# Loads of the conditioning rows moved from SP's queue to POOL's, and the updates of x in three feed-forwards done by adding transfers

## The chip, the cores and the metric

One core of one Trainium2 chip. Measured is the device time in microseconds (us) of one execution; lower is better. Work goes to TensorE (PE, with PEld for its weight loads), VectorE (DVE), ScalarE (ACT), GpSimd (POOL) and to DMA transfers, which a queue of SyncE (SP) or of POOL issues. Each of these runs its own instructions strictly in order.

## The reference, cut to what matters

Two layers over 640 tokens (128 context, 512 latent) of width 1024. Each layer is a feed-forward, a token mixing and a second feed-forward; every one of the three has its own shift, scale and gate, which come from a conditioning vector:

```python
mods = (silu(cond) @ w_ada + b_ada).reshape(cond.shape[0], 9, 1, 1024)
sh1, sc1, g1, sh2, sc2, g2, sh3, sc3, g3 = [mods[:, i] for i in range(9)]
...
h = modulate(rmsnorm(x, p['norm_ffn1']), sh1, sc1)
x = x + 0.5 * g1 * swiglu(h, p['w_ffn1_in'], p['w_ffn1_out'])
```

`swiglu(h, w_in, w_out)` is `(silu(g) * u) @ w_out` with `g, u` the halves of `h @ w_in`, 2816 columns each. `cond` differs between context and latent tokens, so every row of `w_ada` is multiplied with two vectors.

## The kernel before, in words

x lies transposed in SBUF as eight tiles `x` of 128 channels by 640 tokens. Every product is made three times, with a high and a low half of both factors: `Weights.piece` (L168 to L176) rounds a loaded weight tile `raw` to `hi` on ACT (L174) and takes the rest `lo` on DVE (L175). There are four `hi` and four `lo` buffers and nine `raw` buffers; SP loads the `raw` tiles (L159).

**A feed-forward** (`ffn`, L532) goes through 22 column pairs in five parts of 5, 5, 4, 4 and 4 (`PARTS`). In a part first come the *pairs* (`pair`, L596): seven products of combined blocks (PE, L503), with four sums of weight tiles (DVE, L608), evictions and the activation. Then comes the *out part*: for each of the eight x tiles `out` (L644) multiplies the part's activations with `w_out` (PE, L135) and `x_update_joined` (L523) adds the product times the gate to x, with two DVE instructions (L528, 128 and 512 columns). This text calls the four feed-forwards F1 to F4 (layer 0 first, layer 0 second, layer 1 first, layer 1 second), the pairs of their parts P1 to P5 and the out parts O1 to O5. In the first part of F1 two pairs are done in another way (`plain_pair`), and in the last out part of each feed-forward the next norm's tiles are made as well (`nx.tile`).

**The conditioning rows.** `ada_steps` (L258) makes 128 rows of the product with `w_ada` in one *step*: a 512 KB load into one of two `wa` buffers (L268) and two DVE instructions with a running sum (L270), one for each conditioning vector. A list of such steps, the `Pump`, is filled ahead of F1, F2 and F3 (`ada_all`), and `tick` (L538) takes a step from it whenever a credit, which grows by 2 times a rate for a pair and by the rate for an x tile, has reached one. `RATES` gives the rate of each feed-forward; F4 has none. There are 132 steps. Written order is not final: a scheduler orders the instructions of each engine when the program is built, so an instruction may stand earlier or later in its engine's row than its place in the code.

The evictions `g` and `u` of a pair, and from the change on the products for x, come from one pool of five buffers, `T` (tiles named `t`). PSUM has two buffers `S` for the products of the out part.

Of the kernel before, what the change touches and what calls it, by code (L numbers as in the profile page):

```python
# [12 lines left out]
AF = mybir.ActivationFunctionType  # L13
ALU = mybir.AluOpType
# [8 lines left out]
POOLD = ()  # L23
SHO = range(8)
SPREAD = 3
RATES = (0.8, 0.8, 0.55)
WLATE = 4
P1A, P0B, P1B = 1, 2, 2
D = 1024
# [3 lines left out]
N = NC + NL  # L33
TX = N + 2
FFN = 2816
NP = 22
# [11 lines left out]
HN = N // 2  # L48
# [3 lines left out]
SEGS = ((0, 0, NC), (1, NC, N))  # L52
# [30 lines left out]
def hybrid_step(ctx: ExitStack, tc: tile.TileContext, x_in, cc_in, cb_in, w_ada0, w_ada, pv_in, lam_in, w_fin, w_fout, w_min, w_mout,  # L83
                cache_in, ident_in, rope_in, cnt_in, sel_in,
                y_out, ngk, ngv, ndk, ndv):
    nc = tc.nc
    V, S, G, PE = nc.vector, nc.scalar, nc.gpsimd, nc.tensor
# [13 lines left out]
    def nm(s):  # L101
        uid[0] += 1
        return f"{s}_{uid[0]}"
# [4 lines left out]
    def T(dt=F32):  # L108
        return tp.tile([128, UW], dt, tag="t", name=nm("t"))
# [11 lines left out]
    def PS():  # L121
        return psS.tile([128, 2, 512], F32, tag="S", name=nm("S"))

    def PH():
        return psH.tile([128, 512], F32, tag="H", name=nm("H"))

    def PF():
        return psF.tile([128, 512], F32, tag="F", name=nm("F"))

    def C(shape, dt=F32, name="c"):  # L130
        n = nm(name)
        return const.tile(shape, dt, tag=n, name=n)
# [5 lines left out]
    x = [C([128, N], name="x") for _ in range(KT)]  # L138
# [11 lines left out]
    def raw_tile():  # L150
        return wp.tile([128, 512], F32, tag="raw", name=nm("raw"), bufs=RAWB)

    def load_raw(src):

        n, r = src.shape[-1], []
        for c in range(0, n, 512):
            w = min(512, n - c)
            t = raw_tile()
            nc.sync.dma_start(t[:, :w], src[:, c:c + w])  # L159
            r.append(t[:, :w])  # L160
        return r

    class Weights:
# [5 lines left out]
        @staticmethod  # L169
        def piece(src, eng=None):  # L170
            n = src.shape[-1]
            hi = wp.tile([128, 512], F32R, tag="hi", name=nm("hi"), bufs=HLB)
            lo = wp.tile([128, 512], F32R, tag="lo", name=nm("lo"), bufs=HLB)
            S.activation(hi[:, :n], src, AF.Copy)  # L174
            (eng or V).tensor_tensor(out=lo[:, :n], in0=src, in1=hi[:, :n], op=ALU.subtract)  # L175
            return hi, lo  # L176
# [45 lines left out]
    mods = [[None] * 18 for _ in range(L)]  # L222

    def bada(l, c):
        b = PV_BADA + l * 72 + 4 * c
        return pv[:, b:b + 4].unsqueeze(2).to_broadcast([128, 4, 2])
# [33 lines left out]
    def ada_steps(l, c):  # L260
        m = []

        def step(b):
            if b == 0:
                m.append(C([128, 4, 2], name="mod"))
            t = sp.tile([128, 1536], F32, tag="KS", name=nm("wa"), bufs=2)
            raw, dump = t[:, :D], t[:, D:].bitcast(mybir.dt.bfloat16)
            nc.sync.dma_start(raw, w_ada[l, 4 * c + b])  # L268
            for i, o in enumerate((dump, raw)):
                V.scalar_tensor_tensor(out=o, in0=raw, scalar=1.0, in1=rows[i], op0=ALU.mult, op1=ALU.mult,  # L270
                                       accum_out=m[0][:, b, i:i + 1])
            if b == 3:
                V.tensor_tensor(out=m[0], in0=m[0], in1=bada(l, c), op=ALU.add)
                mods[l][c] = m[0]

        return [lambda b=b: step(b) for b in range(4)]
# [10 lines left out]
    def gate_tiles(l, sub):  # L287

        if sub == 1:
            return [mods[l][2 * (3 * sub + 2) + h] for h in range(2)]  # L290
        r = []
        for h in range(2):
            t = C([128, 4, 2], name="gate")
            V.tensor_scalar(out=t, in0=mods[l][2 * (3 * sub + 2) + h], scalar1=-0.5, scalar2=None, op0=ALU.mult)
            r.append(t)
        return r
# [199 lines left out]
    def product(ps, piece, act, start):  # L496

        hi, lo = piece
        for k in range(4):
            w0, w1 = hi[:, k * 128:(k + 1) * 128], lo[:, k * 128:(k + 1) * 128]  # L500
            ah, al = act[k][:, 0], act[k][:, 1]
            for p, (w_, a) in enumerate(((w0, ah), (w0, al), (w1, ah))):
                PE.matmul(ps, w_, a, start=start and k == 0 and p == 0, stop=k == 3 and p == 2, skip_group_check=True)  # L503
# [20 lines left out]
    def x_update_joined(d, p, gate):  # L524
        g = gate[d // 4]
        w = p.rearrange("p a b -> p (a b)")[:, 512 - HN:512 - HN + N]
        for c, a, b in SEGS:
            V.scalar_tensor_tensor(out=x[d][:, a:b], in0=w[:, a:b], scalar=g[:, d % 4, c:c + 1], in1=x[d][:, a:b],  # L528
                                   op0=ALU.mult, op1=ALU.add)


    def ffn(l, sub, norm, nxt, pump, prate):  # L532
        wi = w_fin[l * 2 + (0 if sub == 0 else 1)]
# [65 lines left out]
        def pair(i, first):  # L599


            a11, a12 = load_raw(wi[i, 0])
            a21, a22 = load_raw(wi[i, 1])
            s3 = raw_tile()
            piece = Weights.piece

            def add(o, a, b):
                V.tensor_tensor(out=o, in0=a, in1=b, op=ALU.add)  # L608

            A, B, D = PF()[:, :HW], PH()[:, :HW], PS()[:, 0, :HW]  # L610
            g, u = T(), T()
            w = piece(a11)
            product(A, w, norm.get("B11"), True)
            S.activation(g[:, :HW], A, AF.Copy)
            w = piece(a12)
            add(s3, a11, a21)
            add(a21, a21, a22)
            add(a11, a21, a11)
            product(B, w, norm.get("B21"), True)
            if first:  # L620
                norm.stats_sum()
            V.tensor_tensor(out=g[:, :HW], in0=B, in1=g[:, :HW], op=ALU.add)
            w = piece(a11)
            product(A, w, norm.get("N2"), False)
            S.activation(u[:, :HW], A, AF.Copy)
            w = piece(s3)
            add(a12, a11, a12)
            product(D, w, norm.get("T3"), True)
            S.activation(u[:, HW:], D, AF.Copy)
            if first:  # L630
                norm.stats_spread()
            w = piece(a21)
            product(A, w, norm.get("N1"), False)
            V.tensor_tensor(out=u[:, HW:], in0=A, in1=u[:, HW:], op=ALU.add)
            w = piece(a22)
            product(D, w, norm.get("T4"), False)
            V.tensor_tensor(out=u[:, :HW], in0=D, in1=u[:, :HW], op=ALU.add)
            w = piece(a12)
            product(A, w, norm.get("B22"), False)
            V.tensor_tensor(out=g[:, HW:], in0=A, in1=norm.R[:, HW:], op=ALU.mult)  # L640
            V.tensor_tensor(out=g[:, :HW], in0=g[:, :HW], in1=norm.R[:, :HW], op=ALU.mult)
            V.tensor_tensor(out=u, in0=u, in1=norm.R, op=ALU.mult)  # L642
            activation(i, g, u, HN)

        def out(k0, k1, d, gate, nx):
            ps = PS()
            w = load_w(wo[d, :, k0 * 128:k1 * 128])
            mm3(joined(ps), CN, w, acts[k0:k1], range(k1 - k0))
            x_update_joined(d, ps, gate)
            if nx is not None:  # L650
                nx.tile(d)
            tick(1.0)
# [55 lines left out]
        gate = None  # L708
        for k0, k1 in PARTS:
            for i in range(k0, k1):  # L710
                if l == 0 and sub == 0 and i < NPLAIN:
                    plain_pair(i)
                    if i == 0:
                        for k in range(4):
                            norm.late(k)
                else:
                    pair(i, i == 0)
            gate = gate or gate_tiles(l, sub)
            nx = nxt() if k1 == NP else None
            if k1 == NP and nx is None:  # L720
                last_out(k0, k1, gate)
            else:
                for d in ORDER:
                    out(k0, k1, d, gate, nx)
# [677 lines left out]
    nx = FastNorm(0, 0)  # L1402
# [24 lines left out]
    pump = Pump()  # L1427

    def ada_all(l, cs):
        for c in cs:  # L1430
            pump.add(ada_steps(l, c))

    ada_all(0, (4, 5, 8, 9, 6, 7, 10, 11, 14, 15, 12, 13))
    nx = ffn(0, 0, nx, lambda: Norm(0, 1), pump, RATES[0])
    pump.step(1000)
    cache = load_cache(0)
    lambdas()
    nx = mix(0, nx, lambda: FastNorm(0, 2), cache)
    cache = load_cache(1)
    rows = silu_rows()  # L1440
    ada_all(0, (16, 17))
    ada_all(1, (2, 3, 0, 1, 4, 5, 8, 9, 6, 7))
    nx = ffn(0, 2, nx, lambda: (pump.step(8), FastNorm(1, 0))[1], pump, RATES[1])
    pump.step(1000)
    ada_all(1, (10, 11, 14, 15, 12, 13, 16, 17))
    nx = ffn(1, 0, nx, lambda: Norm(1, 1), pump, RATES[2])
    pump.step(1000)
    nx = mix(1, nx, lambda: FastNorm(1, 2), cache)
# [113 lines left out]
```

## Time and profile before

| | |
|---|---|
| runs | 2492.87, 2497.93 and 2497.96 us; median 2497.93 |
| profiled execution | 2492.2 us; its span, first to last instruction, 2490.4 us; mean granted clock 0.977 |
| busy, share of the span | PE 95%, PEld 92%, DVE 85%, ACT 49%, POOL 13% |
| DMA | 280.70 MB, 113 GB/s on the mean; all of it from SP's queue, but for 2.70 MB of instructions |

"Busy" is the time in which an engine has an instruction under way; the shares are means over stages that differ. A window row of the trace gives, for one stretch, each engine's busy time with the number of its instructions, the granted TensorE clock (1.00 is 2.4 GHz), and the mean share and rate of the 16 DMA engines. Where an engine's busy time is as long as the stretch, it had no pause there. The chain that ended last is nearly all PE in the part of the span that the page shows.

### The profile page before, as it was taken

The numbers are of one execution on the slowest core, as the hardware profiler recorded it, in microseconds if no ns is written. First come the engines' busy times: TensorE is split into PE (matmuls) and PEld (weight loads), VectorE is DVE, ScalarE is ACT, GpSimd is POOL, SyncE is SP. The second block draws the span as 40 slices with busy tenths as digits, with TensorE's granted clock in tenths as the row PEclk, the third lists the DMA queues.
The fourth block names the chain that finished last, engine by engine and source line by source line (L and its number), as shares of the span: only waits on it lengthen the run. The fifth ranks groups of instructions, "written<-read, shape, count | busy, mean of one in ns | idle before, by whom it ended". The sixth has DMA issues, their size and how long they took to land. (4 is left out here: it accounts for less than half of the span.)

```text
span 2490.4 us, 42262 instructions
## 1 busy us (share of the span) xinstructions
PE 2360.5 (95%) x15497; PEld 2290.3 (92%) x15497; DVE 2108.2 (85%) x3978; ACT 1213.3 (49%) x2447; POOL 315.2 (13%) x373
## 2 busy tenths in 40 slices
PE   7799999999998999998989999999999989999998
PEld 4798998999988899998979999999998979999997
DVE  5999998867887999999999998778588688767776
ACT  3534333457664634334355344445576565434434
POOL 3100000034233100000030000002422330000002
PEclk8999999999999999999989999999999989999999
DMA  7354443223423144554423453222243112223223
GB/s 267 109 169 139 156 156 117 86 80 122 136 75 123 60 153 125 160 161 147 128 81 104 155 150 96 69 85 85 76 154 105 51 39 80 82 78 97 81 73 98
DMA packets 142671, 280.70 MB, mean 113 GB/s; under 512 B 15360, under 2 KB 33664, under 8 KB 142464
## 3 DMA queue, kind: packets, MB, share of 16 engines
q1 hardware_dynamic: 142464, 278.01, 35.0%
q8 instruction: 122, 2.00, 0.3%
q14 instruction: 85, 0.70, 0.1%
HBM read 263.00 MB, written 14.94 MB: 112 GB/s over the span
## 5 line engine op out<-in xcount | busy, mean ns | idle before, releaser
L174 ACT ACTIVATE hi<-raw 128x512 fp32r<-128x512 f32 (+2 forms) x954 | 569.3, 605 | 874.2 <-PE S L135 359.4
L503 PE MATMUL F<-u,hi 128*128 128x322 f32 x2752 | 634.7, 318 | 33.0 <-ACT hi L174 31.1
L175 DVE TENSOR_TENSOR lo<-raw,hi 128x512 fp32r<-128x512 f32 (+1 forms) x874 | 565.2, 659 | 114.2 <-ACT hi L174 110.4
L135 PE MATMUL S<-u,hi 128*128 128x320 f32 (+3 forms) x2144 | 485.2, 317 | 35.5 <-DVE x L517 12.9
L503 PEld LDWEIGHTS F<-u,hi 128*128 128x128 f32 x2752 | 469.3, 192 | 41.7 <-ACT hi L174 34.3
L503 PE MATMUL F<-u,lo 128*128 128x322 f32 x1376 | 432.9, 315 | 10.5 <-DVE lo L175 10.5
L135 PE MATMUL S<-u,lo 128*128 128x320 f32 (+3 forms) x1776 | 419.3, 312 | 3.2 <-DVE lo L175 2.3
L135 PEld LDWEIGHTS S<-u,hi 128*128 128x128 f32 x2144 | 361.4, 193 | 46.9 <-issue 13.3
L270 DVE SCALAR_TENSOR_TENSOR wa<-wa,sc 128x1024 bf16<-128x1024 f32 (+1 forms) x264 | 323.5, 1233 | 9.7 <-DMA wa<-in_w_ada_dram 6.3
L135 PE MATMUL S<-e,hi 128*128 128x320 f32 (+2 forms) x1408 | 327.8, 310 | 1.1 <-DVE e L197 0.8
L503 PE MATMUL S<-u,hi 128*128 128x322 f32 x1376 | 316.1, 315 | 2.6 <-DVE x L528 2.3
L135 PEld LDWEIGHTS S<-u,lo 128*128 128x128 f32 x1776 | 305.1, 191 | 4.5 <-DVE lo L175 3.3
L503 PEld LDWEIGHTS F<-u,lo 128*128 128x128 f32 x1376 | 267.0, 194 | 13.8 <-DVE lo L175 13.1
L608 DVE TENSOR_TENSOR raw<-raw,raw 128x512 f32<-128x512 f32 x344 | 239.7, 697 | 5.2 <-DMA raw<-in_w_fin_dram 2.1
L135 PE MATMUL F<-u,hi 128*128 128x320 f32 (+1 forms) x1056 | 239.2, 318 | 1.5 <-DVE x L517 0.8
L503 PEld LDWEIGHTS S<-u,hi 128*128 128x128 f32 x1376 | 234.2, 191 | 5.7 <-ACT hi L174 5.0
L135 PEld LDWEIGHTS S<-e,hi 128*128 128x128 f32 x1408 | 236.6, 188 | 2.9 <-DVE e L197 2.5
L503 PE MATMUL S<-u,lo 128*128 128x322 f32 x688 | 215.3, 313 | 1.4 <-DVE lo L175 1.4
L528 DVE SCALAR_TENSOR_TENSOR x<-S,gate,x 128x128 f32<-128x128 f32 (+1 forms) x304 | 152.6, 544 | 53.0 <-PE S L135 52.1
L135 PEld LDWEIGHTS F<-u,hi 128*128 128x128 f32 x1056 | 178.6, 193 | 3.9 <-DVE x L517 0.8
L135 PE MATMUL F<-u,lo 128*128 128x320 f32 (+1 forms) x528 | 157.8, 318 | 0.0
L503 PE MATMUL H<-u,hi 128*128 128x322 f32 x688 | 156.0, 313 | 1.7 <-ACT hi L174 1.7
(229 smaller groups left out, 3032.8 us busy)
## 6 DMA issues: line engine op xcount, KB each, us to landing
raw<-in_w_fin_dram SPq DMA_DIRECT2D x352, 256.0 KB
wa<-in_w_ada_dram SPq DMA_DIRECT2D x132, 512.0 KB
raw<-in_w_fout_dram SPq DMA_DIRECT2D x168, 256.0 KB
raw<-in_w_min_dram SPq DMA_DIRECT2D x72, 256.0 KB
u<-in_w_ada_dram SPq DMA_DIRECT2D x24, 256.0 KB
KS<-kd SPq DMA_DIRECT2D x16, 384.0 KB
raw<-in_w_mout_dram SPq DMA_DIRECT2D x24, 256.0 KB
kd<-t SPq DMA_DIRECT2D x8, 640.0 KB
```

The source lines that it names most:

```text
L135: PE.matmul(out, lhsT, rhs, start=start, stop=stop)
L174: S.activation(hi[:, :n], src, AF.Copy)
L175: (eng or V).tensor_tensor(out=lo[:, :n], in0=src, in1=hi[:, :n], op=ALU.subtract)
L270: V.scalar_tensor_tensor(out=o, in0=raw, scalar=1.0, in1=rows[i], op0=ALU.mult, op1=ALU.mult, accum_out=m[0][:, b, i:i + 1])
L503: PE.matmul(ps, w_, a, start=start and k == 0 and p == 0, stop=k == 3 and p == 2, skip_group_check=True)
L528: V.scalar_tensor_tensor(out=x[d][:, a:b], in0=w[:, a:b], scalar=g[:, d % 4, c:c + 1], in1=x[d][:, a:b], op0=ALU.mult, op1=ALU.add)
L608: V.tensor_tensor(out=o, in0=a, in1=b, op=ALU.add)
```

## The change

Five edits. (1) The 512 KB loads of `ada_steps` are issued by POOL and no longer by SP. (2) In F1, F2 and F3 the out parts O1 to O4 call a new function `x_update_dma`: ACT multiplies the product in PSUM with the gate into a `t` tile (two instructions), and POOL issues a 320 KB transfer from that tile which adds to the x tile in SBUF. O5 and all of F4 keep the two DVE instructions. (3) `RATES` goes from 0.8, 0.8, 0.55 to 0.6, 0.42, 0.6. (4) Four groups of rows (16 steps) go from the list of F2 to that of F3. (5) Ahead of the first gate the pump is run until the gate's rows are there.

```diff
-RATES = (0.8, 0.8, 0.55)
+RATES = (0.6, 0.42, 0.6)
...
-            nc.sync.dma_start(raw, w_ada[l, 4 * c + b])
+            G.dma_start(raw, w_ada[l, 4 * c + b])
...
+    def x_update_dma(d, p, gate):
+        g = gate[d // 4]
+        w = p.rearrange("p a b -> p (a b)")[:, 512 - HN:512 - HN + N]
+        t = T()
+        for c, a, b in SEGS:
+            S.activation(t[:, a:b], w[:, a:b], AF.Copy, scale=g[:, d % 4, c:c + 1])
+        G.dma_start(x[d], t[:, :N], accum_op=ALU.add)
...
-            x_update_joined(d, ps, gate)
+            (x_update_dma if k1 < NP and prate else x_update_joined)(d, ps, gate)
...
+            while gate is None and mods[l][2 * (3 * sub + 2) + 1] is None:
+                pump.step()
             gate = gate or gate_tiles(l, sub)
...
-    ada_all(1, (2, 3, 0, 1, 4, 5, 8, 9, 6, 7))
-    nx = ffn(0, 2, nx, lambda: (pump.step(8), FastNorm(1, 0))[1], pump, RATES[1])
+    ada_all(1, (2, 3, 0, 1, 4, 5))
+    nx = ffn(0, 2, nx, lambda: (pump.step(1000), FastNorm(1, 0))[1], pump, RATES[1])
     pump.step(1000)
-    ada_all(1, (10, 11, 14, 15, 12, 13, 16, 17))
+    ada_all(1, (8, 9, 6, 7, 10, 11, 14, 15, 12, 13, 16, 17))
```

The instructions of DVE, in the order in which the built programs have them, hold this many L270 instructions (two to a step) in each stretch, P1 of F1 with all that stands ahead of it:

| | P1 | O1 | P2 | O2 | P3 | O3 | P4 | O4 | P5 | to the next P1 |
|---|---|---|---|---|---|---|---|---|---|---|
| F1 before | 25 | 14 | 15 | 13 | 13 | 12 | 12 | 0 | 0 | 11 |
| F1 now | 22 | 20 | 11 | 18 | 8 | 16 | 8 | 1 | 0 | 11 |
| F2 before | 6 | 14 | 15 | 13 | 13 | 12 | 13 | 9 | 8 | 3 |
| F2 now | 6 | 19 | 10 | 19 | 8 | 16 | 8 | 16 | 8 | 3 |
| F3 before | 8 | 12 | 11 | 12 | 0 | 0 | 0 | 0 | 0 | 0 |
| F3 now | 8 | 18 | 10 | 0 | 0 | 0 | 0 | 0 | 0 | 0 |

Three places show what moved. The first is DVE in O3 of F1; `lo` is a weight tile of the out part, `wa` a conditioning load with its two vectors `sc_319` and `sc_322`, `x` an x tile. Before:

```order
L175 TENSOR_TENSOR lo_3537<-raw_3534,hi_3536 128x512
L270 SCALAR_TENSOR_TENSOR wa_3566,mod_3528<-wa_3566,sc_319 128x1024
L175 TENSOR_TENSOR lo_3574<-raw_3571,hi_3573 128x512
L528 SCALAR_TENSOR_TENSOR x_82<-S_3495,gate_1256,x_82 128x128
L528 SCALAR_TENSOR_TENSOR x_82<-S_3495,gate_1256,x_82 128x512
L270 SCALAR_TENSOR_TENSOR wa_3566,mod_3528<-wa_3566,sc_322 128x1024
```

and with the change:

```order
L175 TENSOR_TENSOR lo_3622<-raw_3619,hi_3621 128x512
L270 SCALAR_TENSOR_TENSOR wa_4334,mod_4182<-wa_4334,sc_319 128x1024
L175 TENSOR_TENSOR lo_3657<-raw_3654,hi_3656 128x512
L270 SCALAR_TENSOR_TENSOR wa_4334,mod_4182<-wa_4334,sc_322 128x1024
L270 SCALAR_TENSOR_TENSOR wa_4373,mod_4182<-wa_4373,sc_319 128x1024
L175 TENSOR_TENSOR lo_3697<-raw_3694,hi_3696 128x512
```

The two x instructions are gone and conditioning instructions stand in their place, between the same weight tiles.

The second is the queue of loads at the same O3. Before, SP's row (`raw` with `w_fin` are weights of the next pairs):

```order
L268 DMA wa_3529<-in_w_ada_dram 128x1024
L268 DMA wa_3566<-in_w_ada_dram 128x1024
L159 DMA raw_3720<-in_w_fin_dram 128x512
L159 DMA raw_3722<-in_w_fin_dram 128x512
L268 DMA wa_3603<-in_w_ada_dram 128x1024
L268 DMA wa_3640<-in_w_ada_dram 128x1024
```

and with the change POOL's:

```order
L268 DMA wa_4183<-in_w_ada_dram 128x1024
L268 DMA wa_4334<-in_w_ada_dram 128x1024
L538 DMA x_81<-t_3461 128x640
L538 DMA x_85<-t_3496 128x640
L268 DMA wa_4373<-in_w_ada_dram 128x1024
L538 DMA x_82<-t_3535 128x640
L268 DMA wa_4412<-in_w_ada_dram 128x1024
```

SP has only weights there now; on POOL a conditioning load and the addition to an x tile take turns, each behind the one ahead of it.

The third is the start of the program. Before, SP issues the first conditioning loads behind the x tiles and the vectors `sc`, and ahead of the `u` tiles:

```order
L255 DMA sc_319<-in_cb_dram 128x1024
L255 DMA sc_322<-in_cb_dram 128x1024
L268 DMA wa_326<-in_w_ada_dram 128x1024
L268 DMA wa_330<-in_w_ada_dram 128x1024
L247 DMA u_303<-in_w_ada_dram 128x512
```

and with the change they are POOL's first transfers:

```order
L1397 MEMSET u_101 128x512
L268 DMA wa_326<-in_w_ada_dram 128x1024
L268 DMA wa_330<-in_w_ada_dram 128x1024
L469 MEMSET R_484 128x2x2
L310 MEMSET shc_5294 128x32
```

Two loads of 512 KB moved from behind SP's first 32 transfers to the very start, on the other queue.

## Rows read from the trace of the kernel before

**Rows 1.** The page: the span, and each engine's busy time.

```profile
span 2490.4 us, 42262 instructions
...
PE 2360.5 (95%) x15497; PEld 2290.3 (92%) x15497; DVE 2108.2 (85%) x3978; ACT 1213.3 (49%) x2447; POOL 315.2 (13%) x373
```

**Rows 2.** Windows: start:end, length, PE, PEld, DVE, ACT, POOL busy, clock, DMA.

```profile
167.82:235.82 68.00, 63.56 (x424) 62.55 (x423) 67.56 (x123) 33.24 (x65) 0.00 (x0) 1.00 0.40 123
235.82:272.04 36.22, 35.38 (x241) 34.86 (x240) 35.66 (x76) 9.35 (x20) 0.00 (x0) 1.00 0.61 192
272.04:327.53 55.49, 52.00 (x340) 51.41 (x339) 55.09 (x100) 26.68 (x51) 0.00 (x0) 0.97 0.46 145
327.53:356.47 28.94, 28.34 (x193) 27.89 (x192) 28.04 (x54) 5.78 (x9) 0.00 (x0) 1.00 0.42 132
...
417.07:445.10 28.03, 28.03 (x195) 28.03 (x194) 18.82 (x36) 6.62 (x11) 0.34 (x2) 1.00 0.18 57
...
926.78:996.21 69.43, 65.05 (x424) 64.07 (x423) 67.63 (x122) 33.30 (x64) 0.85 (x3) 0.98 0.38 120
...
1117.19:1177.83 60.64, 53.76 (x340) 51.65 (x339) 59.18 (x107) 26.89 (x54) 0.00 (x0) 0.97 0.48 154
1177.83:1206.48 28.65, 28.27 (x192) 28.04 (x192) 28.25 (x53) 6.49 (x11) 0.00 (x0) 1.00 0.45 142
```

**Rows 3.** The same view for P2, O2, P4 and O4 of F3.

```profile
1403.57:1466.30 62.73, 62.73 (x424) 62.71 (x423) 62.06 (x113) 33.06 (x64) 1.95 (x4) 1.00 0.37 114
1466.30:1501.40 35.10, 35.10 (x242) 35.10 (x240) 34.19 (x69) 9.19 (x19) 0.18 (x3) 1.00 0.56 173
...
1580.23:1630.73 50.50, 50.50 (x340) 50.17 (x339) 41.60 (x72) 27.08 (x51) 0.00 (x0) 1.00 0.34 100
1630.73:1659.00 28.27, 28.27 (x192) 28.01 (x192) 18.32 (x33) 6.45 (x11) 0.00 (x0) 1.00 0.15 47
```

**Rows 4.** Windows of L270 alone: DVE busy (instructions, reads of the sum counted).

```profile
167.82:235.82 68.00, 16.90 (x28) 1.00 0.40 123
235.82:272.04 36.22, 17.14 (x28) 1.00 0.61 192
272.04:327.53 55.49, 15.84 (x26) 0.97 0.46 145
327.53:356.47 28.94, 13.46 (x23) 1.00 0.42 132
...
1117.19:1177.83 60.64, 16.86 (x28) 0.97 0.48 154
1177.83:1206.48 28.65, 12.15 (x20) 1.00 0.45 142
```

**Rows 5.** Windows of L528 alone: DVE busy in O1 to O4 of F3.

```profile
1312.13:1709.48 397.35, 32.23 (x64) 1.00 0.36 111
```

**Rows 6.** Timeline of ACT: an eviction of a whole tile's width.

```profile
101.00 0.73 ACT L548 ACTIVATE t<-t 128x514 f32<-128x514 f32 x1 [3.71 <-DVE t L640]
```

**Rows 7.** Timeline of SP's queue at the start: start, time to issue, count.

```profile
1.19 3.74 SPq L247 DMA_DIRECT2D u<-in_w_ada_dram  x8
...
43.35 1.48 SPq L268 DMA_DIRECT2D wa<-in_w_ada_dram  x2
```

**Rows 8.** Timeline of DVE, with the idle time ahead and its end.

```profile
46.95 1.23 DVE L270 SCALAR_TENSOR_TENSOR wa<-wa,sc 128x1024 bf16<-128x1024 f32 x1 [2.48 <-DMA wa<-in_w_ada_dram]
```

**Rows 9.** Groups of POOL by line: busy us, mean ns, idle before.

```profile
L318 POOL TENSOR_TENSOR t<-t,t 128x640 f32<-128x640 f32 x42 | 77.7, 1850 | 113.9 <-ACT t L316 113.2
```

**Rows 10.** Timeline of DVE: one form, inside a POOL addition and just ahead of one.

```profile
1267.28 1.86 DVE L443 TENSOR_TENSOR t<-t 128x322 f32<-128x322 f32 x1
...
1301.44 0.49 DVE L443 TENSOR_TENSOR t<-t 128x322 f32<-128x322 f32 x1 [1.45 <-POOL t L318]
```

**Rows 11.** Timeline of POOL: the addition that runs at 1267.

```profile
1266.70 2.10 POOL L318 TENSOR_TENSOR t<-t,t 128x640 f32<-128x640 f32 x1 [7.10 <-ACT t L316]
```

**Rows 12.** Window of the start, all engines.

```profile
10.00:33.00 23.00, 18.44 (x57) 8.60 (x55) 14.56 (x25) 12.61 (x28) 9.14 (x5) 0.85 1.04 399
```

## The prediction

> **What bounds the kernel now.** I read the page first: PE is busy 95% of the span, DVE 85% [rows 1]. By that share alone nothing moved off DVE would matter. But a share is a mean over stages, so I read the windows next, one for each stretch of a feed-forward. In P2, O2 and P3 of F1 the long engine is DVE: busy 67.56 of 68.00 us, 35.66 of 36.22, 55.09 of 55.49, while PE has pauses (63.56, 35.38 and 52.00); in O3 both are at the end of it (28.34 and 28.04 of 28.94), and F2 looks like F1 [rows 2]. In F3, with fewer conditioning rows, PE is busy for the whole stretch and that is the floor: 62.73 us for pairs of a five-pair part, 35.10 for its out part, 50.50 and 28.27 for a four-pair part [rows 3]; O4 of F1, which holds no conditioning work, lies at the floor before the change (28.03) [rows 2].
>
> From this the excess: P2 to O4 of F1 run from 167.82 to 445.10, 277.28 us. The floor for the same six stretches is 62.73 + 35.10 + 2 x (50.50 + 28.27) = 255.37. So 21.9 us are lost there. In F2, from 926.78 to 1206.48, it is 279.70 - 255.37 = 24.3 [rows 2, 3]. Together 46.2 us: what the change can win. F3 and F4 stand at the floor and can win nothing.
>
> **Does DVE fit under PE after the change?** One L270 instruction costs 16.90/14 = 1.21 us in P2 of F1 (28 rows there are 14 instructions and 14 reads of their sums) [rows 4]. The x updates of four out parts cost 32.23 us, 8.06 for one [rows 5]. What DVE has to do in each kind of stretch without L270 is its busy time less the L270 share [rows 2, 4], and to that I add the number of L270 that the change's table puts there:
>
> - Five-pair part, pairs: 67.56 - 16.90 = 50.7; with 11 it is 64.0, with 10 62.8, against 62.73. Just full in F1, even in F2 and F3.
> - Its out part: 35.66 - 17.14 = 18.5, less 8.06 for x, plus 18 to 20 at 1.21: 32.2 to 34.6, against 35.10. Fits.
> - Four-pair part, pairs: 55.09 - 15.84 = 39.3 or, by F2's row, 59.18 - 16.86 = 42.3; with 8 it is 48.9 to 52.0, against 50.50. Full.
> - Its out part: 28.04 - 13.46 = 14.6 or 28.25 - 12.15 = 16.1, less 8.06, plus 16 x 1.21: 25.9 to 27.4, against 28.27. Fits.
>
> So DVE is loaded to 91 to 103% of PE's floor everywhere. The sums over the floor are 1.2 us (P2 of F1) and up to 1.5 in each of five P3 and P4 stretches, 8.7 at most; at the least 1.2 is left. I take 5, since two queues that are both full never mesh without a gap. **Term A: 46.2 - 5 = -41 us** (bounds -37.5 and -45).
>
> **What takes the x updates.** ACT gets 16 instructions in an out part. Two cover the 640 columns of one tile, and an eviction of 128x514 takes 0.73 us [rows 6], so at most 2 x 0.73 x 8 = 12 us on top of 9.35 busy of 36.22 in O2 [rows 2]: ACT is idle beside it, and this is hidden. If that cover went (ACT late with `hi`), PE would wait for PSUM `S`, which is now freed by ACT. The `t` tiles come from five buffers, and the next pair's evictions take from the same five. Each x tile has about 4 us of PE (35.10/8), so an addition may be late by about four tiles before ACT's next `t` waits. The five-buffer limit is thus hidden unless POOL's queue stalls as a whole. The next part's x update of the same tile is a whole part later.
>
> **The start.** Two 512 KB loads now come first. From 10 to 33 us the DMA engines are full: share 1.04 at 399 GB/s [rows 12]. So 1.05 MB more ahead of the first weights is 1.05/0.399 = 2.6 us later for PE. Against that, in P1 of F1 DVE has three L270 fewer (25 to 22), 3.6 us, where DVE is late, and SP's queue no longer stops behind a load whose `wa` buffer is taken: its next two loads of conditioning rows are issued at 43.35 us only [rows 7]. **Term B: +1 us** (bounds -4 and +6).
>
> **POOL's queue.** Not one transfer of POOL's is in the trace of before, so its price has to be bounded. All of POOL's DMAs stand in one row, a `wa` load behind an addition to x and that behind a `wa` load, and there are only two `wa` buffers. A step's cycle: at 43.35 a `wa` load is issued on SP and at 46.95 its first L270 starts, after waiting for the load [rows 7, 8]: 3.60 us, then two L270, 2.41: 6.0. Two buffers can serve a step each 3.0 us. What is asked: 8 steps in 28.27, 3.53 each, or up to 9.5 (mean of O1 and O2) in 35.10, 3.69 each. So the cycle may grow by e = 2 x 3.53 - 6.0 = 1.06 us, or 1.4, before DVE waits; beyond it each step costs (e - room)/2. Such out parts hold 24 steps of the one kind (O3 of F1, O3 and O4 of F2) and 47 of the other (O1, O2 of F1 and F2, O1 of F3). Lower end of e: 0, by SP's issue of eight loads in 3.74 us, 0.47 each, which the 3.60 already holds [rows 7]. Upper end: POOL takes for a transfer as long as for its slowest work in the trace, 1.85 us [rows 9], with one such transfer ahead in the queue: 3.70 - 0.47 = 3.2 us; then 24 x 2.14/2 + 47 x 1.8/2 = 68 us. I choose e = 1.5, in the middle: writing a transfer's list is work on an engine, so nearer to POOL's 1.85 [rows 9] than to SP's 0.47, but most loads would not find an addition just ahead of them. **Term C: 24 x 0.44/2 + 47 x 0.1/2 = +8 us** (bounds 0 and +68). The Trainium skill gives, in "DMA: Bandwidth & Descriptors", section Specifications, about 1 us to the first byte from POOL's queue and about 0.6 from SP's; by that e would be 0.4 and Term C nothing, and the time some 8 us less than mine (an estimate). No run here shows it yet.
>
> A second price of POOL's: it may slow DVE. One DVE form of 128x322 took 1.86 us where it began inside POOL's addition, and 0.49 where it did not [rows 10, 11]. That is +1.37 us, from an addition that reads two tiles; a transfer that POOL issues reads none in the program. I count nothing, with 0 and 1.37 as ends. The Trainium skill ("SBUF — State Buffer", section Who interferes with whom) says that a DVE instruction with two SBUF inputs stands in the way of a POOL instruction that reads SBUF, not of one that only writes, and infers that issuing a transfer needs the write side only. By this rule the price is nothing too; by the row alone, at one hit for each of the 71 loads and 64 additions of these out parts, 135 transfers, it would be +185 us, and the rival below bears it.
>
> **Sum.** -41 + 1 + 8 = -32. The profiled execution took 2492.2 us, so 2460; the shown runs go from 2492.87 to 2497.96 with a median 5.7 above the profiled one. I put half of that on top: **2463 us**.
>
> **The rivals.**
>
> 1. *DVE waits for conditioning loads in the out parts.* O2 of F1 moves 192 GB/s now [rows 2]. With 2.5 more steps of 0.524 MB and eight additions of 0.328 MB, 3.9 MB in 35.1 us, it is about 305 GB/s, and 380 if the reading of x by the addition counts too; the start shows that 399 is full [rows 12]. Then loads take longer than the 3.60 us. With e = 2.0: 24 x 0.94/2 + 47 x 0.6/2 = 25 us instead of 8: 2480 (2475 to 2490). For: the bursts fall in the same stretches. Against: the mean is far below full. Chance 0.13.
> 2. *POOL's queue sets the pace: slower than before.* A load waits for a free `wa` buffer at the head of the queue, the additions stand behind it, ACT gets no `t`, PE no `S`. In a four-pair out part POOL has 16 transfers in 28.27 us, so above 1.77 us for one transfer it is the bound by itself; and Term C eats all of the 41 - 1 from e of 2.4 us on. Toward e = 3.2 it gives 2492 - 41 + 1 + 68 = 2520 (2500 to 2530). For: the 1.85 us [rows 9]. Against: that is arithmetic over 640 columns, and the issue of a transfer touches none. Chance 0.12.
> 3. *POOL slows DVE.* DVE is at the floor everywhere, so every microsecond counts; at 41/135 = 0.3 us a transfer all is given back, at 0.6 it is 2500 and over. The 1.86 us [rows 10, 11] speaks for it, the kind of instruction against. Chance 0.04.
> 4. *No change.* The steps are not spread as `RATES` asks, since the scheduler places them: L270 bunch in out parts (16 to 20 each), and both engines being full they do not mesh; or a floor that only F3's DVE load allows. Of the excess 46 then 40 stay: 2488 to 2503. Chance 0.07.
>
> **How the numbers follow.** The forecast, 2448 to 2475, has 0.64 and its likeliest time is 2463; the rivals have 0.13, 0.12, 0.04 and 0.07. A measurement of this kernel tells about 0.2%, 5 us, from no change. Faster: forecast and rival 1, 0.64 + 0.13 = 0.77. Same: rival 4, 0.07. Slower: rivals 2 and 3, 0.16. The range leaves out no more than 2 in 10: low end 2444, which is Term C at 0, Term A at -45 and B at -3; high end 2500, which takes in rival 1 and most of rival 4. Outside lie rivals 2 and 3 and a little of the forecast's edge.
>
> **What would show it.** Right: P2 to O4 of F1 and F2 within about 3 us of 255.37 each, PE without pauses there, DVE at 91 to 103% of each stretch; ACT's two new instructions some 1.2 us together, and none waiting for a buffer. Term B: PE's first matmul on the first weights some 2 to 3 us later. Term C: idle time of DVE ahead of L270 that ends with a `wa` load, 8 us in all; rival 1 has 25 or more, with the DMA share near 1 in out parts. Rival 2 shows PE or ACT waiting for the addition to x, and POOL's queue with transfers longer than 1.8 us. Rival 3 shows the same DVE forms longer in out parts than before. Rival 4 shows stretches as long as before at fewer DVE microseconds. I am wrong above all if a POOL transfer costs much more than SP's 0.47 us, or if the additions to x take so long that the next part finds x late.

## The result, and the profile after

The change made the kernel slower: 2526.85 us median of four runs (2523.21 to 2528.43) against 2495.4 (2491.99 to 2497.96), a ratio of 1.0125 with a 95% interval of 1.0106 to 1.0144. The forecast was 2463 us with a range of 2444 to 2500, so the time lies outside the range and on the other side. The profiled execution took 2526.54 us.

The page of the changed kernel, its lines on the span, the engines, the two queues and POOL's transfers:

```profile
span 2524.8 us, 42654 instructions
...
PE 2372.8 (94%) x15497; PEld 2298.1 (91%) x15497; DVE 2026.9 (80%) x3786; ACT 1296.0 (51%) x2639; POOL 464.8 (18%) x601
...
q0 software_dynamic: 32832, 100.68, 15.6%
...
L270 DVE SCALAR_TENSOR_TENSOR wa<-wa,sc 128x1024 bf16<-128x1024 f32 (+1 forms) x264 | 325.6, 1236 | 76.7 <-DMA wa<-in_w_ada_dram 72.5
...
wa<-in_w_ada_dram POOLq DMA_DIRECT2D x132, 512.0 KB, 4.6
...
x<-t POOLq DMA_DIRECT2D x96, 320.0 KB, 5.7
```

Against [rows 1] DVE lost 81 us of work (the 96 moved updates come to 97 us at the price of [rows 5]), and the span grew by 34 us all the same. The line to read is that of L270: ahead of the conditioning instructions DVE stood idle for 76.7 us, 72.5 of them for a `wa` load. Before, it was 6.3, and the forecast allowed 8 more:

```profile
L270 DVE SCALAR_TENSOR_TENSOR wa<-wa,sc 128x1024 bf16<-128x1024 f32 (+1 forms) x264 | 323.5, 1233 | 9.7 <-DMA wa<-in_w_ada_dram 6.3
```

The windows of P2 to O4 of F1, then O1 and P5 of F2 and P2 of F3 (columns as in [rows 2]):

```profile
174.19:242.09 67.90, 64.60 (x424) 64.06 (x423) 67.84 (x124) 34.95 (x68) 4.99 (x8) 0.97 0.45 134
242.09:281.62 39.53, 37.02 (x241) 36.55 (x241) 28.95 (x59) 14.95 (x32) 9.71 (x14) 0.96 0.87 232
281.62:336.60 54.98, 51.38 (x340) 50.07 (x339) 54.91 (x99) 27.20 (x54) 4.95 (x8) 1.00 0.52 157
336.60:366.49 29.89, 28.42 (x192) 27.91 (x192) 23.02 (x42) 12.22 (x25) 8.16 (x12) 1.00 0.72 197
366.49:426.85 60.36, 53.96 (x340) 52.91 (x339) 56.13 (x102) 27.67 (x53) 5.67 (x14) 0.94 0.54 156
426.85:455.35 28.50, 28.21 (x193) 27.88 (x192) 14.45 (x24) 12.16 (x25) 6.59 (x10) 1.00 0.55 122
...
903.04:946.26 43.22, 38.44 (x241) 37.78 (x240) 33.09 (x64) 15.65 (x33) 11.13 (x16) 0.92 0.86 233
...
1223.88:1282.66 58.78, 53.98 (x340) 53.19 (x339) 55.30 (x100) 27.67 (x53) 5.30 (x9) 0.94 0.54 156
...
1436.01:1504.15 68.14, 65.75 (x424) 64.32 (x423) 65.78 (x119) 34.23 (x67) 4.55 (x10) 0.97 0.43 124
```

P2 to O4 of F1 take 455.35 - 174.19 = 281.2 us, more than before (277.3) and not the floor of 255.4. P2 and P3 are still full of DVE (67.84 of 67.90 us in P2). The out parts, where DVE was to be full as well, show the opposite: in O2 it works 28.95 us of 39.53. There the DMA engines are busy 0.87 of the time, at only 232 GB/s. Three stretches that stood at the floor before the change no longer do: O1 and P5 of F2, whose rows before are these, and P2 of F3 [rows 3].

```profile
891.78:926.78 35.00, 35.00 (x241) 34.99 (x240) 34.58 (x69) 9.32 (x19) 0.00 (x0) 1.00 0.58 191
...
1206.48:1256.72 50.24, 50.24 (x340) 50.21 (x339) 49.45 (x92) 26.48 (x51) 0.00 (x0) 1.00 0.43 138
```

Who waits in O1 of F2, by the waits of DVE, then of PE (us in total, times, longest):

```profile
DVE wa L270 <- DMA wa<-in_w_ada_dram: 8.3, 5, 3.8
...
PE S L135 <- DVE lo L175: 4.8, 2, 4.4
```

and the place of the longest wait, in DVE's timeline and then in PE's:

```profile
937.70 1.22 DVE L270 SCALAR_TENSOR_TENSOR wa<-wa,sc 128x1024 bf16<-128x1024 f32 x1 [3.79 <-DMA wa<-in_w_ada_dram]
938.85 0.08 DVE L270 DVE_READ_ACCUMULATOR wa<-wa,sc 128x1 f32 x1
938.85 0.89 DVE L175 TENSOR_TENSOR lo<-raw,hi 128x512 fp32r<-128x512 f32 x2
```

```profile
939.59 0.90 PE L135 MATMUL S<-u,lo 128*128 128x320 f32 x2 [4.41 <-DVE lo L175]
```

DVE waits for a conditioning load that PE does not need, the `lo` weights stand behind it in DVE's row, and PE waits for `lo`. The pause costs a second time: after it PE works at a granted clock of 0.50 (1.2 GHz).

```profile
939.59:944.50 4.91, 4.91 (x18) 4.91 (x19) 4.84 (x11) 0.00 (x0) 1.48 (x3) 0.50 0.94 251
```

Of the 8.2 us by which O1 of F2 grew, 4.8 are PE's waits and 3.4 are longer work on the same 241 products (38.44 us at a mean clock of 0.92, against 35.00 at 1.00). Over the whole span PE's busy time grew by 12.3 us, of the 34 that the span did.

### The profile page after: what moved, and what is told of

Same layout as the page of the kernel before. It is cut to its first block, busy times and chain, and to the rows that moved or that the text cites. A ratio compares the mean times of both kernels' runs of the same rounds, so it can differ in the third digit from the quotient of the medians.

```text
span 2524.8 us, 42654 instructions
## 1 busy us (share of the span) xinstructions
PE 2372.8 (94%) x15497; PEld 2298.1 (91%) x15497; DVE 2026.9 (80%) x3786; ACT 1296.0 (51%) x2639; POOL 464.8 (18%) x601
## 3 DMA queue, kind: packets, MB, share of 16 engines
q0 software_dynamic: 32832, 100.68, 15.6%
## 5 line engine op out<-in xcount | busy, mean ns | idle before, releaser
L270 DVE SCALAR_TENSOR_TENSOR wa<-wa,sc 128x1024 bf16<-128x1024 f32 (+1 forms) x264 | 325.6, 1236 | 76.7 <-DMA wa<-in_w_ada_dram 72.5
L268 POOL DMA_DIRECT2D wa<-in_w_ada_dram x132 | 73.1, 554 | 786.1 <-DVE wa L270 754.9
```

Source lines behind the costliest of these rows:

```text
L268: G.dma_start(raw, w_ada[l, 4 * c + b])
```

## The experiments

Thirteen kernels ran, each with the kernel before beside it on the same chip; ratios are to that. "Steps" are conditioning steps as before. Three theories were on trial: A, the additions fill the DMA engines; B, the order on POOL's queue with two `wa` buffers makes loads late; C, moving x off DVE lets the scheduler draw steps together, which costs by itself. (In the first run C stands for something else: POOL's transfers dear by themselves.)

### The loads on POOL alone

```diff
-            nc.sync.dma_start(raw, w_ada[l, 4 * c + b])
+            G.dma_start(raw, w_ada[l, 4 * c + b])
```

> The kernel before with one edit: the loads of the conditioning rows issued by POOL. Theory A (the DMA engines' time: in an out part of the changed kernel the additions to x take about 1.78 us of all 16 engines each, a conditioning load 1.65, the weights 9.8 in all, together about 40 us against 35.1): only 21 us of DMA time in an out part here, so no cost there; about +5 us from the two loads at the start, 2495 to 2503. Theory B (POOL's queue: a load that waits for its buffer holds up what stands behind it): nothing stands behind the loads here, the same 2495 to 2503. Theory C (POOL's transfers are dear by themselves): above 2510.

Measured: 2501.27 us, ratio 1.0021 (1.0012 to 1.0031). O1 of F2 stays at 35.16 us; F1's pairs begin at 82.49 us in place of 77.40. That is as A and B expected, and its theory C is out. By themselves POOL's loads cost the start and nothing in the out parts.

### The additions alone

The kernel before with `x_update_dma` in O1 to O4 of F1 to F3 (and the early gate).

> The kernel before with the additions to x by transfers alone; loads on SP and the rates as before. Theory A: O1 and O2 of F1 and F2 have 9.8 + 7 x 1.65 + 8 x 1.78 = 35.6 us of DMA time against 35.1, so they stay about as long as before or 1 to 4 us longer each, while the pairs gain little: 2485 to 2505. Theory B: loads and additions are on two queues, nothing is held up, and DVE has 8 us less per out part: 2465 to 2480.

Measured: 2508.56 us, ratio 1.0047 (1.003 to 1.0064). Both theories were off: A by 4 us, B by 28 or more. DVE waits 69.2 us for loads although these are on SP's queue, so POOL's order is not what makes them late here:

```profile
L270 DVE SCALAR_TENSOR_TENSOR wa<-wa,sc 128x1024 bf16<-128x1024 f32 (+1 forms) x264 | 325.2, 1236 | 73.0 <-DMA wa<-in_w_ada_dram 69.2
```

### The change with its loads back on SP

> The changed kernel with the loads of the conditioning rows back on SP's queue, the additions alone on POOL's. Theory A: the DMA time of O1 and O2 is as before this edit, so they stay at 39 to 44 us; 2515 to 2530, less 5 at the start. Theory B: O1 and O2 return to 35 to 36 us, 2460 to 2480.

Measured: 2508.87 us, ratio 1.0053 (1.0038 to 1.0068), just under A's range and far above B's. O1 of F2, its window, is between the two as well:

```profile
894.40:931.75 37.35, 35.70 (x242) 35.17 (x241) 30.08 (x60) 15.05 (x31) 6.08 (x7) 1.00 0.89 246
```

43.2 us fell to 37.4, at a DMA share of 0.89 (0.86 in the changed kernel): POOL's order is part of the cost beside the additions (1.0125 - 1.0053, 18 us of 2495, the start included), not its main part. DVE still waits 64.2 us for loads. And the spread, which separates this kernel from the one above, gains nothing while the additions are there.

### The change with x back on DVE

```diff
-            (x_update_dma if k1 < NP and prate else x_update_joined)(d, ps, gate)
+            x_update_joined(d, ps, gate)
```

> The changed kernel with the x updates back on DVE; loads on POOL and the spread as changed. Theory A: DMA time in O1 falls to 9.8 + 9.5 x 1.65 = 25.5 us, the wait for loads goes; DVE has 18.5 + 19 x 1.21 = 41.5 us in O1 where the floor is 35.1, but 4 to 5 us less in the pairs; with 16 steps moved from F2 to F3 2475 to 2500. Theory C (the bunching of steps in out parts costs, not the transfers): O1 and O2 stay at 40 to 44 us and the whole at 2515 or more.

Measured: 2462.72 us, ratio 0.9864 (0.9849 to 0.988): faster than A hoped. With x on DVE fewer L270 run in O1 than the 19 that A had assumed (14 in O1 of F2), and the waits for loads are down to 9.8 us.

### The spread alone

> The changed kernel without the additions and with the loads back on SP's queue: the kernel before with the new rates, the moved groups and the early gate alone. With x on DVE and loads on POOL it took 2462.7 us. Theory A (the additions' DMA time is what costs, the loads on POOL cost about 5 us at the start and nothing else): 2452 to 2462, with the first product on the weights as early as before. Theory B (the order on POOL's queue matters also without the additions): the same or less by up to 3 us more. Rival (POOL's loads helped, since SP's queue stops less for a buffer): 2465 to 2475.

Measured: 2452.67 us, ratio 0.9832 (0.9815 to 0.9848). As A expected. This is faster than the kernel before and than the changed one. The windows of P2 to O4 of F1:

```profile
168.65:231.01 62.36, 62.36 (x422) 62.36 (x421) 62.26 (x113) 33.23 (x63) 0.00 (x0) 1.00 0.37 113
231.01:266.34 35.33, 35.33 (x243) 35.03 (x241) 35.02 (x75) 9.90 (x22) 0.00 (x0) 1.00 0.63 193
266.34:316.62 50.28, 50.28 (x338) 49.90 (x337) 49.79 (x89) 26.56 (x50) 0.00 (x0) 1.00 0.46 137
316.62:346.51 29.89, 28.54 (x195) 28.05 (x193) 29.44 (x56) 6.56 (x11) 0.00 (x0) 1.00 0.51 156
346.51:396.38 49.87, 49.87 (x339) 49.87 (x337) 49.47 (x90) 26.84 (x50) 0.00 (x0) 1.00 0.43 132
396.38:424.50 28.12, 28.12 (x195) 28.09 (x193) 27.73 (x52) 6.56 (x11) 0.00 (x0) 1.00 0.46 146
```

PE has no pause but in O3; the six take 255.9 us against the forecast floor of 255.4, and those of F2 257.5. O1 of F1, which has more steps than before, takes 42.9 us against 35; the gain lies behind it. Where the steps went shows in windows of L270 alone (DVE busy, instructions with reads), O3, O4 and P5 of F1 in this kernel:

```profile
316.62:346.51 29.89, 12.91 (x23) 1.00 0.51 156
...
396.38:424.50 28.12, 12.16 (x20) 1.00 0.46 146
424.50:478.90 54.40, 9.80 (x16) 0.97 0.38 121
```

and P3, O3, P4 and O4 in the changed kernel:

```profile
281.62:336.60 54.98, 13.44 (x22) 1.00 0.52 157
336.60:366.49 29.89, 14.58 (x23) 1.00 0.72 197
366.49:426.85 60.36, 14.91 (x26) 0.94 0.54 156
426.85:455.35 28.50, 2.46 (x4) 1.00 0.55 122
```

Same rates, yet the changed kernel has nearly nothing left for O4 and holds 14.91 us of L270 in P4, where the spread alone holds 9.30. The loads on POOL are not the reason: with them, but x back on DVE, O4 and P5 of F1 hold as much as with the spread alone:

```profile
399.61:427.69 28.08, 12.18 (x20) 1.00 0.46 149
427.69:482.09 54.40, 9.81 (x16) 0.97 0.40 121
```

### A copy in place of the addition

```diff
-        G.dma_start(x[d], t[:, :N], accum_op=ALU.add)
+        G.dma_start(x[d], t[:, :N])
```

> The changed kernel with the transfer to x as a plain copy that adds nothing (x is overwritten by the product, so the values of the output are other ones). Theory A with the adding itself as the dear part: a copy of 0.328 MB at some 300 GB/s takes 1.1 us of the DMA engines in place of 1.78, O1 has 9.8 + 15.7 + 8.8 = 34.3 us of DMA time, and O1 of F2 falls from 43.4 to 36 to 39 us, the whole to 2500 to 2512. Theory A with the size as the dear part (two ends in SBUF): 1.7 to 1.8 us a copy and 2520 to 2530. Theory B: the queue is as before, 2520 to 2530 with copies of 1.1 us.

Measured: 2505.64 us, ratio 1.0039 (1.0024 to 1.0054); O1 of F2 fell to 36.54 us: as theory A with the adding as the dear part expected. The price of one transfer can be read in O2 of F3, where no conditioning load runs beside it. POOL's queue and its transfers there, first as additions (a stretch of 35.48 us), then as copies (35.50 us):

```profile
q0 software_dynamic: 973, 2.25, 35.1%
...
x<-t POOLq DMA_DIRECT2D x7, 320.0 KB, 4.2
```

```profile
q0 software_dynamic: 560, 2.29, 15.9%
...
x<-t POOLq DMA_DIRECT2D x7, 320.0 KB, 3.5
```

35.1% of 35.48 us over seven transfers is 1.78 us of all 16 engines for one addition, 184 GB/s; a copy of the same bytes takes 15.9% of 35.50 over seven, 0.81 us. The adding is the dear part. An addition also goes as 144 packets (32,832 less 19,008 for the loads, over 96) and a copy as 80, and POOL's issue took 0.90 us for the one and 0.54 for the other. Whether the add itself or the finer cut is what costs was not tried. In the same O2 of F3 the additions cost PE nothing: 35.48 us, with PE busy throughout. They cost where loads run beside them.

### POOL adds by an instruction

```diff
-        G.dma_start(x[d], t[:, :N], accum_op=ALU.add)
+        G.tensor_tensor(out=x[d], in0=x[d], in1=t[:, :N], op=ALU.add)
```

> The changed kernel with POOL adding ACT's product to x by one instruction in place of the transfer; no additions on the DMA engines, and the 18 to 20 conditioning instructions of an out part stay. Theory A: DMA time in O1 falls to 9.8 + 9.5 x 1.65 = 25.5 us, DVE no longer waits for loads, O1 and O2 at 35 to 37 us, the whole at 2450 to 2468. Theory B: POOL's 8 additions of 1.85 us or more stand between the loads and keep them late, O1 at 39 to 44. Theory C (so many conditioning instructions in an out part do not mesh): O1 at 39 to 44 too, but without waits for loads. Rival: POOL's additions slow DVE, its forms of two tiles take longer in the out parts than in the changed kernel, 2480 or more.

Measured: 2549.27 us, ratio 1.0208 (1.0193 to 1.0224). The rival held, so this run could not tell A from C. DVE's forms in O2 of F1, here and then in the changed kernel:

```profile
L270 DVE SCALAR_TENSOR_TENSOR wa<-wa,sc 128x1024 bf16<-128x1024 f32 x8 | 11.5, 1439 | 0.1
...
L175 DVE TENSOR_TENSOR lo<-raw,hi 128x128 fp32r<-128x128 f32 x7 | 8.9, 1270 | 0.0
```

```profile
L270 DVE SCALAR_TENSOR_TENSOR wa<-wa,sc 128x1024 bf16<-128x1024 f32 x8 | 9.8, 1222 | 7.9 <-DMA wa<-in_w_ada_dram 7.9
...
L175 DVE TENSOR_TENSOR lo<-raw,hi 128x128 fp32r<-128x128 f32 x7 | 2.0, 284 | 0.0
```

A `lo` of 128x128 takes 1270 ns in place of 284: the same effect as in [rows 10, 11].

### Half-size loads, with two and with four places

Half of each `w_ada` row block is loaded and used twice:

```diff
-            G.dma_start(raw, w_ada[l, 4 * c + b])
+            G.dma_start(t[:, :512], w_ada[l, 4 * c + b][:, :512])
+            half = t[:, :512].unsqueeze(1).to_broadcast([128, 2, 512])
```

> The changed kernel with conditioning loads of half the size: 256 KB are loaded and used twice by both instructions, so the other half of the rows is left out and the values are other ones; the number and size of DVE's instructions stay, and so does the order on POOL's queue. Theory A: 9.8 + 9.5 x 0.83 + 14.2 = 31.9 us of DMA time in O1 and O2, which fall to 36 to 38 us, the whole at 2490 to 2508. Theory B: each load is as late as its place in the queue makes it, 39 to 43 us, the whole above 2512.

Measured: 2494.25 us, ratio 0.9993 (0.9983 to 1.0002); O1 of F2 36.42 us at a DMA share of 0.69. As A expected. But DVE's wait for loads is still 40.8 us over the kernel. The second of the two puts two steps in one buffer (offset `512 * (b % 2)`), so four loads have a place:

> The run with half-size conditioning loads (2494.3 us, the other half of the rows left out) with four places for loads in place of two: two steps share one buffer. The DMA time is the same as there, so what changes is the cycle of a buffer alone. There DVE still waited 4 to 6 us for loads in each out part though the DMA share was 0.69 to 0.77. Theory A (DMA time alone): the waits stay, 2488 to 2500. Theory B (a load is asked for too late, since only two are under way, and each lands later beside the additions): the waits go, DVE is full in the out parts, the pairs come down to 62.5 and 50 us, and the whole to 2445 to 2470.

Measured: 2475.75 us, ratio 0.9927 (0.9912 to 0.9942), between the two. The wait halves to 20.7 us at the same DMA time. So both act: the engines' time, and the cycle of two buffers as loads land later.

### Slower rates

> The spread alone (2452.7 us) with lower rates, 0.5 and 0.4 in place of 0.6 and 0.42: fewer steps in the first parts of F1, more behind them. O1 of F1 stands at 42.9 us with 18 conditioning instructions and P5 at 54.4 with 8; if the load on DVE sets these, O1 falls to 38 to 41 and the whole to 2444 to 2450; if the steps only move to O5 and the mixing, where PE is the bound as well, 2450 to 2460.

Measured: 2450.40 us, ratio 0.9824 (0.9808 to 0.984). O1 of F1 fell to 39.7 us as expected, and P5 of F1 ended 5.3 us earlier than with the spread alone (473.6 against 478.9). What follows gave it back: the pairs of F4 begin at 1996.6 against 1996.0. From the spread alone (0.9832) the whole cannot be told apart.

### The first loads on SP

> The changed kernel with only the first four conditioning loads back on SP's queue, behind the weights that the start needs. If these loads are what makes the start 5.5 us longer (their 1.05 MB first on full DMA engines, 2.6 us, and what follows from it), F1 begins its pairs at 77 to 78 us in place of 82.9 and the whole is 2519 to 2523. If the start is longer for another reason (the order of the other instructions), it stays at 82 to 83 and 2525 to 2529.

Measured: 2526.11 us, ratio 1.013 (1.0115 to 1.0145): the second case. PE's first product on the weights, in the changed kernel and then here:

```profile
24.06 0.87 PE L135 MATMUL S<-u,hi 128*128 128x320 f32 x2 [2.05 <-ACT hi L174]
```

```profile
22.05 0.56 PE L135 MATMUL S<-u,hi 128*128 128x320 f32 x2 [2.11 <-ACT hi L174]
```

It came 2.0 us earlier, but F1's pairs began at 85.28 us, not at 77 (82.86 in the changed kernel). PE waits 10.4 us for POOL's casts `u` (L416) there, against 8.5 in the changed kernel and 6.1 before. The bytes of the first loads are not why the start is longer. With all loads on SP the pairs begin at 77.05 us (with the additions) and 75.99 (the spread alone), so the longer start does come with POOL's loads. That their issues push POOL's small work back is only argued; it was not tried alone.

### Additions for four of the eight x tiles

> The changed kernel with the additions by transfer for four of the eight x tiles alone, the other four updated by DVE. DMA time in O1: 9.8 + 15.7 + 4 x 1.78 = 32.6 us against 35.1, and DVE has 4 us more to do there. If the cost goes with the number of transfers, about half of the 64 us that the additions cost beside POOL's loads is gone: 2487 to 2500. If a part that is not yet full costs nothing: 2462 to 2475. If any transfer in the queue costs the same, 2515 or more.

Measured: 2480.08 us, ratio 0.9942 (0.9919 to 0.9965), under the first case and over the second. The four are the tiles with d of 4 and more, every second one in the order of the loop. Of the 65 us between the change with x on DVE and the change (1.0125 - 0.9864 of 2495), 46 go when half the additions go, and with them half of the updates return to DVE. Taken together, the two cost more than in proportion to their number; the run cannot part one from the other.

### No addition at all

```diff
-        G.dma_start(x[d], t[:, :N], accum_op=ALU.add)
```

> The changed kernel without the additions to x at all in O1 to O4 of the three feed-forwards: ACT still makes the gated product, nothing adds it, so these eight out parts' share of x is left out. DVE is as free as in the changed kernel and the conditioning steps are drawn together as there, but no transfer stands between the loads. Theory A (the transfers' DMA time): O1 of F2 at 35 to 36 us, DVE's wait for loads falls from 72.5 us to under 20, pairs near 62.7 and 50.5, 2445 to 2465. Theory C (the drawing together of 17 to 20 conditioning instructions in an out part, with two buffers, costs by itself): DVE waits 30 us or more, pairs stay at 55 to 67, 2480 to 2510.

Measured: 2483.03 us, ratio 0.995 (0.9933 to 0.9966), 35.0 us of waits for loads: C's figures, but only for the pairs. P2 and P3 of F1 and O1 of F2:

```profile
169.51:234.73 65.22, 63.14 (x423) 62.35 (x421) 65.20 (x119) 34.68 (x67) 2.65 (x5) 1.00 0.40 118
...
270.41:325.92 55.51, 51.35 (x338) 49.85 (x337) 54.60 (x98) 27.54 (x53) 2.78 (x6) 1.00 0.46 139
...
885.29:920.46 35.17, 35.17 (x242) 35.16 (x241) 31.88 (x63) 15.06 (x31) 4.24 (x8) 1.00 0.69 217
```

Without the transfers O1 of F2, with 18 L270, is at the floor, as A said. The pairs are not: P2 to O4 of F1 take 266.9 us against 255.9 with the spread alone and 255.6 with x on DVE and the loads on POOL. O4 of F1 holds as little L270 as in the changed kernel, and P5 none:

```profile
406.83:436.36 29.53, 2.45 (x4) 1.00 0.16 52
```

So it is x off DVE that draws the steps together, with or without transfers. A and C both hold, for different stretches.

### The account

Each kernel's ratio times 2495.4 us, one edit added at a time (each step is good to about 5 us, and the sizes hold for this order of adding):

| | ratio | against before | this step |
|---|---|---|---|
| spread (edits 3, 4, 5) | 0.9832 | -41.9 us | -41.9 us |
| and loads on POOL | 0.9864 | -33.9 | +8.0 |
| and x off DVE, not added | 0.995 | -12.5 | +21.5 |
| and copied to x | 1.0039 | +9.7 | +22.2 |
| and added to x: the change | 1.0125 | +31.2 | +21.5 |

The copies cost 22 us although an out part with them asks for less engine time than it lasts (31 us of 35.1, as an estimate: 9.4 for the weights, 9.5 loads of 1.6 and 8 copies of 0.81). So the engines need not be full on the mean for a loss. How the 22 us split between POOL's order and loads that land later is open.

## Why the prediction was wrong

Two steps failed. Term A took it that DVE's work would run where the table puts it once x was off DVE's row; that move cost 21.5 us in place of being part of the gain. Terms B and C put the loads on POOL and the transfers at +1 and +8 us; they cost 51.7 (8.0 + 22.2 + 21.5 by the account). That lies inside Term C's own bounds of 0 and 68, so what failed there is the size that was chosen, and the range, which ended at 2500, left the upper part of these bounds out.

- **What bounds the kernel: right.** DVE bound most of P2 to O4 of F1 and F2, and the floor was 255.4 us: the spread alone reached 255.9 and 257.5.
- **Term A, the -41 us: the gain is there, but was put down to the wrong edit.** The spread alone brings -42 with x on DVE. In hindsight the forecast's own prices allow it: 18.5 + 14 x 1.21 = 35.4 us in an out part with 14 L270 and x on DVE, about the floor. The step "I add the number of L270 that the change's table puts there" failed. The table gives DVE's row, not when it runs. By the L270 windows P2, P3 and P4 of F1 held 15.09, 13.44 and 14.91 us, some 12, 11 and 12 instructions in place of 11, 8 and 8. That fits DVE's waits for loads in the out parts ahead (8.0 us in O1, 7.9 in O2 and 6.2 in O3), but was not tried alone. The prices themselves held: with 18 L270 and no transfers O1 of F2 took DVE 31.88 us, forecast 32.2 for 18.
- **What the table did show and the forecast passed over:** one L270 in O4 and none in P5 of F1. The steps were not spread as the rates asked; with x off DVE's row the scheduler drew them forward. Rival 4 named this, with x as no part of its cause, and as worth no more than no change.
- **Term C: the right place, the wrong size and in part the wrong cause.** The waits for loads are 72.5 us, against 6.3 before, where the forecast added 8. With no transfer to x at all 35.0 are left. The term's upper end rested on an issue as slow as POOL's 1.85 us [rows 9]; an issue takes 0.55 us for a load and 0.90 for an addition. What grew was the landing: 5.7 us median in O1 of F2 in the changed kernel, 4.0 with x on DVE. Put into the forecast's formula, 5.7 in place of 3.60 (e = 2.1) gives about 29 us, an estimate, so the landing is not the whole of it.
- **Rival 1 had a part of the mechanism and failed in its price.** It counted bytes at 399 GB/s, 0.82 us an addition; measured are 1.78. With loads at about 1.6 us (59.0% of 35.16 us in O1 of F2 with the spread alone, less 9.4 for the weights, over 7) such an out part asks for 9.4 + 9.5 x 1.6 + 8 x 1.78 = 39 us of engines in 35.1. The forecast saw 305 to 380 GB/s "far below full"; the engines were busy 0.86 of the time at 233.
- **Rival 2 named the time, 2500 to 2530, but not the way there, so the fit is luck.** The head of POOL's queue did wait for a `wa` buffer, for 29.8 us of O1 of F2, with additions behind it. But neither ACT nor PE waited there for what stood behind, and POOL issued 16 transfers in 11.13 us of 43.22. In the whole kernel PE waited 3.0 us for ACT's new product. POOL's order adds a part, some 18 us with the start by the run with loads on SP.
- **Rival 3: transfers did not slow DVE.** `lo` of 128x128 took 284 ns in O2 of F1, 282 before. POOL's addition did (1270 ns). By the rule in the Trainium skill ("SBUF — State Buffer", Who interferes with whom) a DVE instruction with two SBUF inputs contends with a POOL instruction that reads SBUF; the two runs agree with it.
- **The cover of ACT: right.** ACT was busy 15.65 of 43.22 us in O1 of F2, and no wait of PE or ACT there is for the new product or a `t` buffer.
- **Term B: within its bounds, and its reason half right.** PE's first product came 2.8 us later (24.06 against 21.24; forecast 2.6). F1's pairs begin 5.5 us later, but its O1 2.7 earlier, since P1 shrank by 8 us.
- **The first byte:** by the Trainium skill ("DMA: Bandwidth & Descriptors", Specifications), with about 1 us to the first byte from POOL's queue and 0.6 from SP's, Term C was nothing. For loads alone the out parts agree: POOL's loads on the kernel before left O1 of F2 at 35.16 us. These figures are no price for an addition's time on the engines, 1.78 us here.

Not tried: full-size loads with a third buffer. What the cycle of two buffers costs is known only for half-size loads, where four places in place of two took the waits from 40.8 to 20.7 us.

## What to carry to other kernels

Before a job moves from a full engine to the DMA engines, price the transfer in engine time, by the share of its queue in a stretch where it runs alone, and add up all queues for the fullest stretch; bytes over the best rate seen are not enough. Work taken off an in-order engine also frees a scheduler to fill the gap with other work, and if that waits for loads, everything behind it waits too. Test the plain edit (rates, order) alone before an edit that moves work is credited with the gain.

## What the runs showed of the hardware

- An adding transfer of 320 KB within SBUF took 1.78 us of the 16 DMA engines, the same transfer as a copy 0.81: 2.2 times. The addition went as 144 packets, the copy as 80.
- POOL issued a 512 KB load in 0.55 us, an adding transfer in 0.90 and the same transfer as a copy in 0.54.
- After a pause of 4.4 us PE's granted clock was 0.50 for the next 4.9 us, and PE's work in that out part grew from 35.0 to 38.4 us.
- A DVE subtraction of 128x128 with both inputs in SBUF took 1270 ns on the mean beside POOL's additions of two SBUF tiles, 284 beside POOL's transfers.
